# A diffusion step on one core: the broadcast of 1/rms pinned behind more products, one more gMLP group ahead, the last root on ScalarE, stores in smaller first pieces

## The chip, the cores and the metric

One core of one Trainium2 chip runs the whole program in one launch. The metric is device microseconds of that core. Of each kernel there are a few timed runs, and beside them one execution recorded by the hardware profiler, whose own time and span the tables name. The engines are called PE (TensorE), DVE (VectorE), ACT (ScalarE), POOL (GpSimd) and SP (SyncE).

## The reference, cut to what matters

128 prompt tokens and 256 latent tokens with 1024 features go through two layers. Layer 0 mixes by attention, layer 1 by a gated MLP in chunks (gMLP); after each mixer comes a gated ConvFFN. Every one of these four blocks begins with an RMS norm that is shifted and scaled by adaLN, and one RMS norm without adaLN ends the program.

```python
def rmsnorm(x, g):
    xf = x.astype(jnp.float32)
    y = xf * lax.rsqrt(jnp.mean(xf * xf, axis=-1, keepdims=True) + EPS)
    return (y * g.astype(jnp.float32)).astype(x.dtype)
...
def chunk_gmlp(h, w_in, g_v, w_s, b_s, w_out):
    ...
    z = jax.nn.gelu(h @ w_in)
    u, vv = jnp.split(z, 2, axis=-1)
    vv = layernorm(vv, g_v).reshape(B, nc, CHUNK, GMLP_GROUPS, GMLP_GROUP_DIM)
    mixed = jnp.einsum('gpq,bnqgc->bnpgc', w_s, vv) + jnp.transpose(b_s)[:, :, None]
    return (u * mixed.reshape(B, T, GMLP_WIDTH)) @ w_out
...
    for l in range(DEPTH):
        ...
        h = modulate(rmsnorm(x, norm_mix_g[l]), sm, cm)
        ...  # mix: attention in layer 0, chunk_gmlp in layer 1
        x = x + gm * mix
        h = modulate(rmsnorm(x, norm_ffn_g[l]), sf, cf)
        x = x + gf * conv_ffn(h, w_ffn_up[l], w_ffn_conv[l], b_ffn_conv[l], w_ffn_down[l])
    y_prompt = rmsnorm(x, norm_final_g)
```

## The kernel before, in words

The residual x is kept feature-major: eight tiles `x[k]` of 128 features by 384 token columns (128 prompt, 256 latent). Weights come from memory in 512 KB units (`load`, L102); ACT makes the rounded high part `hi` (L105) and DVE the rest `lo` (L106). The activations are held the same way, as `hhi` and `hlo`. One `mac` is three products on PE: high by high, low by high, high by low (L112 to L114; the text calls each a product). A block's result builds up in a PSUM bank of one of five pools; `ps_sc` has two banks, `ps_mm` three.

**A norm.** While the last residual tiles come in, ACT squares them (`square`, L289) and DVE adds the squares into `sqacc`. `norm_first` then works as follows. Four weight units are loaded; `sums` (L303) adds `sqacc` over the partitions on PE; `rsqrt` turns the sums into 1/rms `rr` (DVE L329, a power on POOL L331, one Newton step on DVE L333 to L336); `spread` (L322) copies 1/rms to all partitions with three small matmuls against `ident`; ACT copies the bank to `R` (L371). All this time PE runs 32 macs, 96 products of 386 columns, on an x that was scaled but not yet normalised (`early`), so that `late` (L385 and L386, `lt` and `lc`) can multiply their results by `R` afterwards. `modulated` then writes the normalised `hhi` and `hlo` of all eight tiles (DVE L346, ACT L348, DVE L350) for the products that follow. Norm 1 of the prediction is the one ahead of the ConvFFN of layer 0 (near 221 us), norm 2 that of the gMLP (near 497 us), norm 3 that of the ConvFFN of layer 1 (near 713 us); the norm ahead of attention is not touched.

**gMLP.** Four u groups are made from the first products, then all of v. DVE takes the layernorm statistics, `rsqrt` makes 1/std, and twelve DVE instructions normalise v (`vn`, L887). Sixteen groups follow: two banks of `ps_sc` take turns for the mixing matmuls of a group (L912, `ws` by `vn`), DVE reads the bank into `m` (L915), multiplies by the group's u (L919) and splits it. `u_part(g)` is the 24 products and the gelu (L897) of a group's u.

**The end.** After the last products x is squared once more, summed with `ones`, transposed back on PE (L958, 24 transposes into six banks), multiplied by 1/rms (ACT L967, DVE L969) and stored in six pieces of 256 KB, three issued by SP and three by ACT (L970).

Within the body a scheduler places the instructions on the engines by priorities; instructions marked `keep_in_program_order` stay where the program has them on their engine. Each engine works through its own list in order. ACT holds one table of functions at a time; a change of table is an instruction of its own in its list (ACT_TABLE_LOAD). The small vector work of the adaLN modulation (L260 on DVE) and the weight loads are spread through the program.

Of the kernel before, what the change touches and what calls it, by code (L numbers as in the profile page):

```python
# [20 lines left out]
NT = NPR + NSA
GROUPS = ((0, 0, NPR), (1, NPR, NT))
# [17 lines left out]
def backbone(ctx: ExitStack, tc: tile.TileContext, x_in, cond_in, condr_in, b_ada_in, prm_in,  # L40
             ckT_in, cv_in, wsT_in, bs_in, rpb_in, w_ada, w_ada0, w_adaT, w_qk, w_v, w_o, w_gu, w_gv,
             w_gout, w_up, w_down, y_out, skT_out, sv_out):
    nc = tc.nc
# [43 lines left out]
    make_identity(nc, ident)  # L87
    ones = cst.tile([P, P], F32, name="ones")
    nc.vector.memset(ones, 1.0)
    mhalf = cst.tile([P, 4], F32, name="mhalf")  # L90
    nc.vector.memset(mhalf, -0.5)

# [188 lines left out]
    def square(k, tag="t384", apart=True):  # L281

        sq["last"] = None
        if k == 0:
            sq["acc"] = tmp.tile([P, NT], F32, name="sqacc", tag="sqacc")
            nc.scalar.activation(sq["acc"], x[k], AF.Square)
            return
        t = tmp.tile([P, NT], F32, name="t384", tag=tag, bufs=2 if tag == "t384" else 1)
        nc.scalar.activation(t, x[k], AF.Square)  # L289
        if k < KD - 1 or not apart:  # L290
            nc.vector.tensor_tensor(sq["acc"], sq["acc"], t, ALU.add)
        else:
            sq["last"] = t
# [15 lines left out]
    def inverse(ss):  # L309

        v = tmp.tile([P, 4], F32, name="rv", tag="rv", bufs=2)
        return rsqrt(ss[:, 0:6].rearrange("p (b c) -> p b c", c=2)[:, :, 0], v[:, 0:3], 1.0 / D)

    def rms():

        return spread(inverse(sums()))

    def spread(r):

        R = bank(ps_tb)  # L320
        for b in range(3):
            mm = nc.tensor.matmul(R[:, b * P:(b + 1) * P], r[:, b:b + 1].to_broadcast([P, P]), ident,  # L322
                                  start=True, stop=True)
        return R

    def rsqrt(src, v, scale):
# [36 lines left out]
            nc.vector.scalar_tensor_tensor(hlo[:, k, a:b], x[k][:, a:b], g,  # L363
                                           hhi[:, k, a:b].bitcast(F32), ALU.mult, ALU.subtract)

    def norm_first(nxt, units):

        w = [load(u) for u in units]
        Rp = rms()
        R = tmp.tile([P, 512], F32, name="R0", tag="R0")[:, :NT]  # L370
        nc.scalar.copy(R, Rp[:, :NT])  # L371
        ps = [bank(q) for q in (ps_mm, ps_mm, ps_sc, ps_ta)[:len(w)]]
        for k in range(KD):
            for wi, p in zip(w, ps):
                mac(p[:, :NT + 2], wsel(wi, k, slice(0, P)), h(k, slice(0, NT + 2)),
                    k == 0, k == KD - 1)
        for k in range(KD):
            modulated(*nxt, k, R)
        return ps, R
# [427 lines left out]
    def ffn(l, pool, wkp, fill):  # L807
        ahi = [pool.tile([P, NT], F32R, name=f"ahi{i}") for i in range(KF)]
        alo = [pool.tile([P, NT], F32R, name=f"alo{i}") for i in range(KF)]
        allm = slice(0, P)  # L810

        def gate(i, pg, pv):
            g = conv(l, i, pg, wkp, "cg")
            v = conv(l, KF + i, pv, wkp, "cv")
            nc.scalar.activation(g, g, AF.Silu)
            nc.vector.tensor_tensor(g, g, v, ALU.mult)
            nc.scalar.copy(ahi[i], g)
            nc.vector.tensor_tensor(alo[i], g, ahi[i].bitcast(F32), ALU.subtract)

        order = [j for i in range(KF) for j in (i, KF + i)]  # L820
        ps, R = norm_first((l, SF, CF), [w_up[l, j] for j in order[:4]])

        def joined(p):
            t, c = late(p, R, wkp)
            for i, a, b in GROUPS:
                nc.scalar.activation(t[:, a:b], t[:, a:b], AF.Identity, bias=c[:, i:i + 1])
            return t

        for i in range(2):
            gate(i, joined(ps[2 * i]), joined(ps[2 * i + 1]))  # L830
        for n, j in enumerate(order[4:], 4):
            i = n // 2
            w = load(w_up[l, j], 50)
            ps.append(bank(ps_mm if i % 2 == 0 else ps_sc))
            for k in range(KD):
                mac(ps[n][:, :NT], wsel(w, k, allm), h(k), k == 0, k == KD - 1)
            if n % 2:
                gate(i, ps[n - 1], ps[n])
                if fill and 5 <= i < 21 and i % 2:
                    ada_v.run(1)  # L840
        for m in range(KD):
            ada_v.run(2 if fill else 1)
            ps = bank(ps_mm if m % 2 else ps_sc)
            for k0, kn in ((0, 8), (8, 8), (16, 6)):
                w = load(w_down[l, m, :, k0:k0 + kn, :])
                for kk in range(kn):
                    k = k0 + kk
                    mac(ps[:, :NT], wsel(w, kk, allm), (ahi[k], alo[k]), k == 0, k == KF - 1)
            residual(l, GF, m, ps, (1, SM, CM) if l == 0 else None)


    def gmlp(pool, wkp):
# [3 lines left out]
        mv = pool.tile([P, 3, 2], F32, name="mv")  # L856
        mhi = [pool.tile([P, NT], F32R, name=f"mhi{g}") for g in range(NG)]
        mlo = []
        ps, R = norm_first((1, SM, CM), [w_gu[g] for g in range(4)])
        us = []  # L860
        for g in range(4):
            t, c = late(ps[g], R, wkp)
# [28 lines left out]
        def u_part(g):  # L891
            w = load(w_gu[g])
            pu = bank(ps_mm)
            for k in range(KD):
                mac(pu[:, :NT], wsel(w, k, allm), h(k), k == 0, k == KD - 1)
            u = wkp.tile([P, NT], F32, name="u", tag="u", bufs=2)
            nc.scalar.activation(u, pu[:, :NT], AF.Gelu_apprx_tanh)  # L897
            us.append(u)

        u_part(4)
        for g in range(NG):
            if g % 2 == 0:
                ws = wkp.tile([P, 2, P], F32, name="ws", tag="ws")
# [15 lines left out]
                lo4 = pool.tile([P, 4, NT], F32R, name="mlo", tag="q", bufs=5)  # L921
            mlo.append(lo4[:, g % 4, :])
            split(mhi[g], mlo[g], m2)
            if 4 < g + 1 < NG:
                u_part(g + 1)
            if g > 3 and g % 2:
                ada_v.run(1)
        for m in range(KD):
# [22 lines left out]
    with tc.tile_pool(name="fin", bufs=1) as pool:  # L951
        turned = [[bank(q) for q in two] for two in ((ps_ta, ps_ad), (ps_sc, ps_sc), (ps_mm, ps_mm))]

        def turn(ks):
            for k in ks:
                for b in range(3):
                    o = (k % 4) * P
                    tc.keep_in_program_order(nc.tensor.transpose(  # L958
                        turned[b][k // 4][:, o:o + P], x[k][:, b * P:(b + 1) * P], ident))

        r = inverse(sums(True, lambda: turn(range(3))))
        turn(range(3, KD))
        for b in range(3):
            for half in range(2):
                y = pool.tile([P, 512], F32, name=f"y{b}{half}")
                if half:
                    nc.scalar.activation(y, turned[b][half], AF.Copy, scale=r[:, b:b + 1])  # L967
                else:
                    nc.vector.tensor_scalar(y, turned[b][half], r[:, b:b + 1], None, ALU.mult)  # L969
                (nc.sync, nc.scalar)[half].dma_start(y_out[b, :, 512 * half:512 * half + 512], y)  # L970


def _layout(inp):
# [66 lines left out]
```

## Time and profile before

| what | value |
|---|---|
| timed runs | 1000.45 us median of 3 (999.57 to 1000.53) |
| the profiled execution | 1000.85 us, of which 998.0 us is the span from first to last instruction and 2.85 us lies around it |
| PE busy | 982.9 us |
| DVE busy | 797.4 us |
| ACT busy | 476.3 us |
| POOL busy | 15.8 us |
| memory traffic | 172.94 MB, mean 173 GB/s |

The profile's page gives for each engine its busy time and share of the span, and the chain of work that ended last. Below that lie the timeline (every instruction with its start and its duration; in brackets the idle time of its engine before it and what ended it), the list of waits, and windows that sum an engine's busy time over a stretch. Rows that follow each other on an engine are drawn together as "x3" and the like. A matmul's duration of 0.34 us reaches into the next one, since matmuls are pipelined; what a product costs is the distance between two starts.

### The profile page before, as it was taken

The numbers are of one execution on the slowest core, as the hardware profiler recorded it, in microseconds if no ns is written. First come the engines' busy times: TensorE is split into PE (matmuls) and PEld (weight loads), VectorE is DVE, ScalarE is ACT, GpSimd is POOL, SyncE is SP. The second block draws the span as 40 slices with busy tenths as digits, with TensorE's granted clock in tenths as the row PEclk, the third lists the DMA queues.
The fourth block names the chain that finished last, engine by engine and source line by source line (L and its number), as shares of the span: only waits on it lengthen the run. The fifth ranks groups of instructions, "written<-read, shape, count | busy, mean of one in ns | idle before, by whom it ended". The sixth has DMA issues, their size and how long they took to land.

```text
span 998.0 us, 15825 instructions
## 1 busy us (share of the span) xinstructions
PE 982.9 (98%) x5942; PEld 934.9 (94%) x5942; DVE 797.4 (80%) x1652; ACT 476.3 (48%) x846; POOL 15.8 (2%) x31
## 2 busy tenths in 40 slices
PE   8999999999999999999999999999999999999996
PEld 5788888899999999999988899999999999999996
DVE  5668888689998889899899999687698777777552
ACT  4455656558554544333363334333485444443331
POOL 1000000000000000000000000000000000000000
PEclk9999999999999999999999999999999999999999
DMA  9886676442464445677737756465235333435521
GB/s 338 313 292 179 206 233 201 138 148 85 148 190 152 167 148 156 201 220 220 235 105 256 251 174 185 149 204 177 84 106 182 122 126 121 127 114 180 161 72 63
DMA packets 53019, 172.94 MB, mean 173 GB/s; under 512 B 6016, under 2 KB 11152, under 8 KB 52944
## 3 DMA queue, kind: packets, MB, share of 16 engines
q1 hardware_dynamic: 51840, 169.33, 53.2%
q10 hardware_dynamic: 576, 1.31, 0.3%
q0 software_dynamic: 528, 1.32, 0.3%
q8 instruction: 46, 0.75, 0.3%
q14 instruction: 29, 0.24, 0.1%
HBM read 169.31 MB, written 2.62 MB: 172 GB/s over the span
## 4 chain that ended last, share of the span: by engine, by line
PE 94%; DVE 2%; ACT 1%; issue 1%; POOL 1%; DMA 1%; POOLq 0%; SPq 0%; ACTq 0%
PE bank L113 29%; PE bank L114 29%; PE bank L112 29%; PE bank L678 1%; PE bank L629 1%; PE bank L912 1%; PE bank L661 1%; PE bank L155 1%; PE bank L199 1%; POOL ry L331 1%; DMA lo<-in_x 1%; PE bank L322 0%; DVE lo L118 0%; PE bank L303 0%; DVE bank L636 0%
## 5 line engine op out<-in xcount | busy, mean ns | idle before, releaser
L113 PE MATMUL bank<-hlo,hi 128*128 128x384 f32 (+1 forms) x976 | 330.5, 339 | 0.1
L112 PE MATMUL bank<-hhi,hi 128*128 128x384 f32 (+1 forms) x976 | 330.1, 338 | 0.0
L114 PE MATMUL bank<-hhi,lo 128*128 128x384 f32 (+1 forms) x976 | 329.9, 338 | 0.2 <-DVE lo L118 0.2
L105 ACT CAST hi<-st 128x1024 fp32r<-128x1024 f32 (+1 forms) x184 | 189.1, 1030 | 295.3 <-PE bank L113 237.9
L106 DVE TENSOR_TENSOR lo<-st,hi 128x1024 fp32r<-128x1024 f32 (+1 forms) x184 | 220.5, 1198 | 62.5 <-ACT hi L105 62.3
L114 PEld LDWEIGHTS bank<-hhi,lo 128*128 128x128 f32 x976 | 184.1, 189 | 0.7 <-DVE lo L118 0.5
L112 PEld LDWEIGHTS bank<-hhi,hi 128*128 128x128 f32 x976 | 184.0, 189 | 0.8 <-ACT hi L105 0.4
L113 PEld LDWEIGHTS bank<-hlo,hi 128*128 128x128 f32 x976 | 183.4, 188 | 0.6 <-DVE hlo L118 0.3
L114 PE MATMUL bank<-ahi,lo 128*128 128x384 f32 x352 | 118.3, 336 | 0.0
L113 PE MATMUL bank<-alo,hi 128*128 128x384 f32 x352 | 118.3, 336 | 0.0
L112 PE MATMUL bank<-ahi,hi 128*128 128x384 f32 x352 | 118.1, 336 | 0.0
L260 DVE CUSTOM_DVE_ANT_0 junk<-adb,cs 128x1024 bf16<-128x1024 f32 x72 | 87.8, 1219 | 0.5
L260 DVE CUSTOM_DVE_ANT_0 junk<-adw,cs 128x1024 bf16<-128x1024 f32 x56 | 68.3, 1220 | 0.5
L114 PEld LDWEIGHTS bank<-ahi,lo 128*128 128x128 f32 x352 | 66.2, 188 | 0.0
L113 PEld LDWEIGHTS bank<-alo,hi 128*128 128x128 f32 x352 | 66.2, 188 | 0.0
L112 PEld LDWEIGHTS bank<-ahi,hi 128*128 128x128 f32 x352 | 66.2, 188 | 0.0
L112 PE MATMUL bank<-hi,hhi 128*128 128x512 f32 x144 | 58.1, 404 | 0.4 <-ACT hhi L453 0.4
L113 PE MATMUL bank<-lo,hhi 128*128 128x512 f32 x144 | 56.9, 395 | 0.1
L114 PE MATMUL bank<-hi,hlo 128*128 128x512 f32 x144 | 56.7, 394 | 0.0
L394 DVE SCALAR_TENSOR_TENSOR x<-bank,mod,x 128x128 f32<-128x128 f32 x64 | 23.8, 413 | 33.1 <-PE bank L114 33.0
L113 PE MATMUL bank<-mlo,hi 128*128 128x384 f32 x128 | 43.6, 341 | 0.0
L112 PE MATMUL bank<-mhi,hi 128*128 128x384 f32 x128 | 43.3, 338 | 0.0
(180 smaller groups left out, 1299.8 us busy)
## 6 DMA issues: line engine op xcount, KB each, us to landing
st<-in_w_up SPq DMA_DIRECT2D x88, 512.0 KB, 3.6
adb<-in_w_adaT SPq DMA_DIRECT2D x36, 512.0 KB, 4.5
st<-in_w_down SPq DMA_DIRECT2D x32, 512.0 KB, 3.6
adw<-in_w_adaT SPq DMA_DIRECT2D x28, 512.0 KB, 3.6
adw<-in_w_ada SPq DMA_DIRECT2D x24, 512.0 KB, 5.8
st<-in_w_qk SPq DMA_DIRECT2D x16, 512.0 KB, 4.2
st<-in_w_gu SPq DMA_DIRECT2D x16, 512.0 KB, 4.4
st<-in_w_gv SPq DMA_DIRECT2D x16, 512.0 KB, 4.4
```

The source lines that it names most:

```text
L105: nc.scalar.copy(hi[:, :n], st[:, :n])
L106: nc.vector.tensor_tensor(lo[:, :n], st[:, :n], hi[:, :n].bitcast(F32), ALU.subtract)
L112: nc.tensor.matmul(out, a[0], b[0], start=start, stop=False)
L113: nc.tensor.matmul(out, a[0], b[1], start=False, stop=False)
L114: nc.tensor.matmul(out, a[1], b[0], start=False, stop=stop)
L155: nc.tensor.matmul(pa[32 * j:32 * j + 32, 0:P], cond_s[:, 4 * hf + kk, :], w[hf][:, kk, P * q:P * q + P], start=(kk == 0), stop=(kk == 3), ...
L199: nc.tensor.matmul(self.pa[32 * j:32 * j + 32, 0:256], cond_s[:, k, :], t[:, 256 * j:256 * j + 256], start=(k == 0), stop=(k == KD - 1), t ...
L260: tc.keep_in_program_order(nc.vector.tensor_tensor_reduce(self.junk, t, self.cs[c], 1.0, 0.0, ALU.mult, ALU.add, m[:, c:c + 1]))
L331: nc.gpsimd.tensor_tensor(y, v, mhalf[:, :n], ALU.pow)
L394: nc.vector.scalar_tensor_tensor(x[m][:, a:b], ps[:, a:b], mod(l, gate, m, c), x[m][:, a:b], ALU.mult, ALU.add)
L629: nc.tensor.matmul(sc[hh][:, cols], q[qp][HS[hh], qs:qs + P], k[kp][HS[hh], ks], start=i == 0, stop=i == 2)
L661: nc.tensor.transpose((ta[:, o:o + P] if g < 2 else tb[:, o - 512:o - 512 + P]), pr[:, b, g * P:g * P + P], ident)
```

## The change

Four things are changed.

1. `spread` gets a flag that marks its first matmul `keep_in_program_order`, and `norm_first` calls it in the middle of its 32 macs, behind mac number `then`: 18 in norm 1, 10 in norms 2 and 3. Before, it stood ahead of them in the program, and the scheduler placed it where it expected `rr` to be ready.
2. In the gMLP `u_part(5)` is issued ahead of the first mixing as well, every later `u_part` one group sooner, and the `u` tile has three buffers instead of two.
3. The last norm squares `x[7]` in two pieces. Its root is an ACT Sqrt (with a bias tile `eps`), with a reciprocal on DVE and the Newton step behind it, in place of the power on POOL. A Sqrt of one column after the last gate of the second ConvFFN brings the table in ahead of time.
4. The first 128 tokens are written out as two pieces of 256 columns for each half. There are eight stores, seven of them on SP and the last one on ACT.

The diff, without lines that only move names:

```diff
-        nc.scalar.activation(t, x[k], AF.Square)
+        for _, a, b in GROUPS if k == KD - 1 and apart else ((0, 0, NT),):
+            nc.scalar.activation(t[:, a:b], x[k][:, a:b], AF.Square)
...
-    def rms():
-
-        return spread(inverse(sums()))
-
-    def spread(r):
+    def spread(r, pin=False):
...
+            if pin and not b:
+                tc.keep_in_program_order(mm)
...
-    def norm_first(nxt, units):
+    def norm_first(nxt, units, then):
...
-        Rp = rms()
+        r = inverse(sums())
         R = tmp.tile([P, 512], F32, name="R0", tag="R0")[:, :NT]
-        nc.scalar.copy(R, Rp[:, :NT])
...
+                then -= 1
+                if then == 0:
+                    Rp = spread(r, True)
+                    nc.scalar.copy(R, Rp[:, :NT])
...
-        ps, R = norm_first((l, SF, CF), [w_up[l, j] for j in order[:4]])
+        ps, R = norm_first((l, SF, CF), [w_up[l, j] for j in order[:4]], 10 if l else 18)
...
+        if l:
+
+            nc.scalar.activation(root[:, 3:4], ahi[KF - 1].bitcast(F32)[:, 0:1], AF.Sqrt, scale=0.0)
...
-        ps, R = norm_first((1, SM, CM), [w_gu[g] for g in range(4)])
+        ps, R = norm_first((1, SM, CM), [w_gu[g] for g in range(4)], 10)
...
-            u = wkp.tile([P, NT], F32, name="u", tag="u", bufs=2)
+            u = wkp.tile([P, NT], F32, name="u", tag="u", bufs=3)
...
         u_part(4)
+        u_part(5)
...
-            if 4 < g + 1 < NG:
-                u_part(g + 1)
+            if 5 < g + 2 < NG:
+                u_part(g + 2)
...
-        r = inverse(sums(True, lambda: turn(range(3))))
+        ss = sums(True, lambda: turn(range(3)))[:, 0:6].rearrange("p (b c) -> p b c", c=2)[:, :, 0]
         turn(range(3, KD))
...
+        nc.scalar.activation(root[:, 0:3], ss, AF.Sqrt, bias=eps, scale=1.0 / D)
+        nc.vector.tensor_scalar(v, ss, 1.0 / D, EPS, ALU.mult, ALU.add)
+        nc.vector.reciprocal(y0, root[:, 0:3])
+        nc.vector.tensor_tensor(t, y0, y0, ALU.mult)
+        nc.vector.scalar_tensor_tensor(t, t, -0.5, v, ALU.mult, ALU.mult)
+        nc.vector.scalar_tensor_tensor(r, t, 1.5, y0, ALU.add, ALU.mult)
+        pieces = [(0, 0, 256), (0, 256, 512), (1, 0, 512), (2, 0, 512)]
+        for i, (b, c0, c1) in enumerate(pieces):
             for half in range(2):
...
+                q = nc.scalar if half and i == 3 else nc.sync
+                q.dma_start(y_out[b, :, 512 * half + c0:512 * half + c1], y)
```

Line numbers shift a little with the edit: the products are L113 to L115 afterwards, the split of the weights L106 and L107, `spread` L320, `late` L389 and L390, `vn` L894, the mixing L920 and `m` L923.

The order of the instructions moves further than the diff says, since the scheduler places the rest around the pinned ones. Three places follow. In the rows the numbers behind the names are those of buffers: they tell tiles of one name apart.

PE in norm 1, before: the products of the unnormalised x (banks 2662 to 2665 take turns), with the spread of `rr` between two products of one mac.

```order
L114 MATMUL bank_2664<-hhi_131,lo_2634 128x386
L112 MATMUL bank_2665<-hhi_131,hi_2638 128x386
L322 MATMUL bank_2656<-ident_120,rr_2654 128x128 x3
L113 MATMUL bank_2665<-hlo_132,hi_2638 128x386
L114 MATMUL bank_2665<-hhi_131,lo_2640 128x386
```

The same place now (banks 2658 to 2661).

```order
L115 MATMUL bank_2658<-hhi_132,lo_2623 128x386
L113 MATMUL bank_2659<-hhi_132,hi_2627 128x386
L114 MATMUL bank_2659<-hlo_133,hi_2627 128x386
L115 MATMUL bank_2659<-hhi_132,lo_2629 128x386
L320 MATMUL bank_2716<-ident_120,rr_2655 128x128 x3
L113 MATMUL bank_2660<-hhi_132,hi_2633 128x386
```

The spread is row 1179 of PE's list before and row 1187 now, eight products later; between the sums and the spread stood 12 products, and now 20. In norms 2 and 3 there were 8, and now 14.

DVE at the end of norm 1's modulation, before: `lt` and `lc` free the banks of the first products, `hlo` of tile 7 (from `t384_2811`) is written in two pieces, and `lo_2908` and `lo_2955` are low parts of weight units.

```order
L385 TENSOR_TENSOR lt_2824<-bank_2663,R0_2660 128x384
L386 COPY lc_2825<-bank_2663 128x2
L350 SCALAR_TENSOR_TENSOR hlo_132<-t384_2811,mod0_129,hhi_131 128x128
L106 TENSOR_TENSOR lo_2908<-st_2905,hi_2906 128x1024
L350 SCALAR_TENSOR_TENSOR hlo_132<-t384_2811,mod0_129,hhi_131 128x256
L106 TENSOR_TENSOR lo_2955<-st_2952,hi_2953 128x1024
L801 SCALAR_TENSOR_TENSOR cg_2830<-lt_2818,prm_111,cg_2830 128x127
```

The same place now (tile 7 is `t384_2812`, the first of the two weight parts `lo_2909`).

```order
L350 SCALAR_TENSOR_TENSOR hlo_133<-t384_2805,mod0_130,hhi_132 128x256
L350 SCALAR_TENSOR_TENSOR hlo_133<-t384_2812,mod0_130,hhi_132 128x128
L350 SCALAR_TENSOR_TENSOR hlo_133<-t384_2812,mod0_130,hhi_132 128x256
L390 COPY lc_2826<-bank_2659 128x2
L107 TENSOR_TENSOR lo_2909<-st_2906,hi_2907 128x1024
L805 SCALAR_TENSOR_TENSOR cg_2831<-lt_2819,prm_111,cg_2831 128x127
```

The first weight part now stands behind both pieces of `hlo`, and the second behind the `cg` work. On PE the first product that reads `lo_2908` was row 1256, 77 rows behind the spread; the first that reads `lo_2909` is row 1258, 71 rows behind it. A little later on ACT, the cast of the high part `hi_3032` (before, `hi_3031`) stood directly behind the first gate's Silu and now stands behind two more activations that read `lt_2847` and `lc_2848`; its first product on PE was row 1326 and is now row 1282.

PE at the first mixing of the gMLP, now (`bank_6132` collects u 5, `bank_6224` u 6; the mixing of a group is one row of three matmuls).

```order
L115 MATMUL bank_6132<-hhi_132,lo_6129 128x384
L920 MATMUL bank_6163<-ws_6159,vn_5338 128x128 x3
L920 MATMUL bank_6173<-ws_6159,vn_5338 128x128 x3
L113 MATMUL bank_6224<-hhi_132,hi_6219 128x384
L114 MATMUL bank_6224<-hlo_133,hi_6219 128x384
L115 MATMUL bank_6224<-hhi_132,lo_6221 128x384
L113 MATMUL bank_6224<-hhi_132,hi_6219 128x384
L114 MATMUL bank_6224<-hlo_133,hi_6219 128x384
L920 MATMUL bank_6186<-ws_6182,vn_5338 128x128 x3
L920 MATMUL bank_6195<-ws_6182,vn_5338 128x128 x3
```

Before, 41 products stood between the start of the u groups and the first pair of mixings, and 24 between the first and the second pair; now it is 48 and 5. On DVE, two adaLN reductions (L260) and one weight part (L106) stood between 1/std's first Newton step and the twelve `vn`; now none of these do, and one such reduction stands ahead of the statistics' end instead.

More of the change, by code (lines that the diff above doesn't have):

```diff
@@ L89, in backbone @@
     nc.vector.memset(ones, 1.0)
+    root = cst.tile([P, 4], F32, name="root")
     mhalf = cst.tile([P, 4], F32, name="mhalf")
@@ L959, in turn @@
                         turned[b][k // 4][:, o:o + P], x[k][:, b * P:(b + 1) * P], ident))
-        r = inverse(sums(True, lambda: turn(range(3))))
+        ss = sums(True, lambda: turn(range(3)))[:, 0:6].rearrange("p (b c) -> p b c", c=2)[:, :, 0]
         turn(range(3, KD))
-        for b in range(3):
+        eps = tmp.tile([P, 1], F32, name="eps", tag="eps")
+        nc.vector.memset(eps, EPS)
+        v, y0, t, r = (pool.tile([P, 3], F32, name=n) for n in ("v", "y0", "t", "r"))
+        nc.scalar.activation(root[:, 0:3], ss, AF.Sqrt, bias=eps, scale=1.0 / D)
[6 more added lines that the diff above has]
+        for i, (b, c0, c1) in enumerate(pieces):
             for half in range(2):
-                y = pool.tile([P, 512], F32, name=f"y{b}{half}")
+                y = pool.tile([P, c1 - c0], F32, name=f"y{i}{half}")
+                src = turned[b][half][:, c0:c1]
                 if half:
-                    nc.scalar.activation(y, turned[b][half], AF.Copy, scale=r[:, b:b + 1])
+                    nc.scalar.activation(y, src, AF.Copy, scale=r[:, b:b + 1])
                 else:
-                    nc.vector.tensor_scalar(y, turned[b][half], r[:, b:b + 1], None, ALU.mult)
-                (nc.sync, nc.scalar)[half].dma_start(y_out[b, :, 512 * half:512 * half + 512], y)
+                    nc.vector.tensor_scalar(y, src, r[:, b:b + 1], None, ALU.mult)
+                q = nc.scalar if half and i == 3 else nc.sync
+                q.dma_start(y_out[b, :, 512 * half + c0:512 * half + c1], y)
 def _layout(inp):
```

## The prediction

> **What bounds the kernel now.** I read the page first, then the list of waits, the timeline around each place that the diff touches, and a window behind norm 1.
>
> ```profile
> span 998.0 us, 15825 instructions
> ...
> PE 982.9 (98%) x5942; PEld 934.9 (94%) x5942; DVE 797.4 (80%) x1652; ACT 476.3 (48%) x846; POOL 15.8 (2%) x31
> ...
> PE 94%; DVE 2%; ACT 1%; issue 1%; POOL 1%; DMA 1%; POOLq 0%; SPq 0%; ACTq 0%
> ```
>
> PE is busy for 98% of the span and carries 94% of the chain that ends last. No product is removed, so the change can win only where PE stands still, and behind the last product. Where it stands still, the waits of PE name two lines of this change:
>
> ```profile
> PE bank L322 <- DVE rr L336: 1.4, 3, 0.6
> ...
> PE bank L912 <- DVE vn L887: 0.9, 1, 0.9
> ```
>
> In each of three norms the spread (L322) comes up before `rr` is there, 1.4 us together; the first mixing of the gMLP waits 0.9 us for `vn`. That is nearly all there is to win in the body.
>
> **Part 1, norm 1.** The waits in their places:
>
> ```profile
> 221.09 0.33 PE L112 MATMUL bank<-hhi,hi 128*128 128x386 f32 x1
> ...
> 222.03 0.91 PE L322 MATMUL bank<-ident,rr 128*128 128x128 f32 x6 [0.61 <-DVE rr L336]
> ...
> 497.16 0.91 PE L322 MATMUL bank<-ident,rr 128*128 128x128 f32 x6 [0.34 <-DVE rr L336]
> ...
> 713.13 0.91 PE L322 MATMUL bank<-ident,rr 128*128 128x128 f32 x6 [0.42 <-DVE rr L336]
> ```
>
> The cost of a product comes from the window behind norm 1, quoted below: 13.00 us for 75 starts, 0.173 us each; with 386 columns it is nearer 0.175. From 221.09 to 222.03 are 0.94 us where a product takes 0.175, so 0.77 us are lost; the wait in brackets is 0.16 less because it counts from the modelled end. By the same 0.16, norms 2 and 3 lose 0.50 and 0.58. With eight (six) more products ahead, 1.40 (1.05) us of work, the spread no longer waits: all three losses go, 1.85 us.
>
> But the spread was also the start of another chain: R, `modulated`, `late`. It now starts 1.40 us later against PE's products: in norm 1 at 221.09 + 0.175 + 1.40 = 222.67 instead of 222.03, that is 0.64 later by the clock, while PE is 0.77 ahead. Whether this comes back depends on how far ahead of PE the chain runs afterwards.
>
> ```profile
> 232.00:245.00 13.00, 13.00 (x75) 12.73 (x74) 12.91 (x31) 11.53 (x22) 0.00 (x0) 1.00 0.28 93
> ...
> 234.89 1.22 DVE L106 TENSOR_TENSOR lo<-st,hi 128x1024 fp32r<-128x1024 f32 x1
> 236.03 0.48 DVE L350 SCALAR_TENSOR_TENSOR hlo<-t,mod,hhi 128x256 fp32r<-128x256 f32 x1
> 236.16 0.44 PE L114 MATMUL bank<-hhi,lo 128*128 128x384 f32 x1
> ...
> 236.62 0.39 PE L113 MATMUL bank<-hlo,hi 128*128 128x384 f32 x1
> ```
>
> In the window DVE (third figure) works 12.91 of 13 us: it has no idle time in which to catch up. The weight part `lo` ends at 236.11 and its first product starts at 236.16; `hlo` of the last tile ends at 236.51 and its product starts at 236.62. The slack is 0.05 and 0.11 us. A chain that comes 1.40 us later against PE must stop PE here.
>
> How long, from the new order. `lo_2909` stands behind both pieces of `hlo`, so it is later by the second piece's step (236.42 - 236.03 = 0.39) and by the chain's 0.64: 236.11 + 0.39 + 0.64 = 237.14, and its product, row 1258, can start at 237.19. Before, row 1258 started at 236.62 (the L113 row above). PE is thus 0.57 us behind the kernel before instead of 0.77 ahead: of the 0.77, 1.34 has come back.
>
> The next thing late is a cast on ACT.
>
> ```profile
> 236.42 1.22 DVE L106 TENSOR_TENSOR lo<-st,hi 128x1024 fp32r<-128x1024 f32 x1
> ...
> 240.33 0.53 ACT L815 ACTIVATE cg<-cg 128x384 f32<-128x384 f32 x1
> ...
> 240.65 0.15 DVE L386 COPY lc<-bank 128x2 f32<-128x2 f32 x1
> ```
>
> The groups of the stretch from 234 to 245 us give the two `lt` activations (busy us, mean ns):
>
> ```profile
> L826 ACT ACTIVATE lt<-lt,lc 128x256 f32<-128x256 f32 x4 | 2.0, 499 | 0.0
> ...
> L826 ACT ACTIVATE lt<-lt,lc 128x128 f32<-128x128 f32 x4 | 1.6, 390 | 0.0
> ```
>
> DVE's gate work follows 237.14 now and 237.64 before (the second `lo`, 236.42 + 1.22, has left this place), so Silu comes 0.50 earlier, 239.83 to 240.36; the two `lt` activations take about 0.39 + 0.50 less 0.1 of overlap, to 241.15, and the cast of 1.04 follows to about 242.1. Its first product, row 1282, is 24 products behind row 1258: 237.19 + 24 x 0.175 = 241.39. That is a stop of about 0.7 us. Before, that product was row 1326, 44 products (7.7 us) later. PE is then 0.57 + 0.7 = 1.3 us behind. For stops behind that I know only bounds, nothing and the 0.6 by which the chain was late at 237; I take the middle, 0.3. Norm 1: 1.6 us slower, between 0.6 (only the first stop) and 1.9.
>
> **Norms 2 and 3.** The nearest step behind norm 2 is the copy that frees a bank for the v products:
>
> ```profile
> 510.24 0.15 DVE L386 COPY lc<-bank 128x2 f32<-128x2 f32 x1
> ...
> 511.27 0.40 PE L112 MATMUL bank<-hi,hhi 128*128 128x512 f32 x1
> ```
>
> It ends 0.88 us ahead of its product; the chain shifts by 1.05, so 0.2 comes back and 0.3 of 0.50 is won. Behind norm 3 I found no step with less than 1.05 in hand, so 0.6 is won there. Ends for both together: -1.1 and, if all comes back, 0.
>
> **Part 2, gMLP.**
>
> ```profile
> 577.28 0.34 PE L112 MATMUL bank<-hhi,hi 128*128 128x384 f32 x1
> ...
> 579.15 0.17 DVE L329 TENSOR_SCALAR rv<-mv 128x3 f32<-128x3 f32 x1
> ...
> 581.23 0.16 DVE L333 TENSOR_TENSOR rt<-ry 128x3 f32<-128x3 f32 x1 [0.74 <-POOL ry L331]
> ...
> 584.32 0.33 PE L113 MATMUL bank<-hlo,hi 128*128 128x384 f32 x1
> 584.93 5.57 DVE L887 TENSOR_SCALAR vn<-vn,mv,rr 128x512 f32<-128x512 f32 x12
> 585.52 1.62 PE L912 MATMUL bank<-ws,vn 128*128 128x128 f32 x12 [0.88 <-DVE vn L887]
> 586.91 0.42 PE L114 MATMUL bank<-hhi,lo 128*128 128x384 f32 x1
> ...
> 590.40 1.14 DVE L915 SCALAR_TENSOR_TENSOR m<-bank,prm,bs 128x384 f32<-128x384 f32 x2
> ```
>
> From 584.32 to 585.52 are 1.20 us for one product: 1.03 lost. Seven more products ahead (48 against 41) are 1.2 us, and `vn` starts earlier, so this loss goes. What is late next: the second pair of mixings needs a bank of `ps_sc` that `m` of the first pair (L915) must empty, and on DVE `m` stands behind all twelve `vn`. Before, 24 products (4.2 us) lay between the pairs; now five. Counted from the first u product: PE reaches the second pair after 48 x 0.175 = 8.4, the first pair's 586.91 - 585.52 = 1.39 and 5 x 0.175, at 10.7. On DVE `rv` came at 579.15 - 577.28 = 1.87, now about 1.3 later for the reduction ahead of it (the two that have left took 584.93 - 581.23 = 3.70 with one `lo` of 1.14 among them, so 1.28 each); `rt` 2.08 later as before, two small steps 0.4, then 5.57 of `vn` and 0.57 of one `m`: 11.8. PE stops for about 1.1 us. Gain 1.03, loss 1.1: 0.1 slower, between -1.03 (no stop) and +0.5.
>
> **Parts 3 and 4, the end.**
>
> ```profile
> 988.75 0.16 DVE L329 TENSOR_SCALAR rv<-bank 128x3 f32<-128x3 f32 x1 [1.48 <-PE bank L303]
> ...
> 990.33 0.16 DVE L336 SCALAR_TENSOR_TENSOR rr<-rt,ry 128x3 f32<-128x3 f32 x1
> 990.59 1.26 ACT L967 ACTIVATE y<-bank,rr 128x512 f32<-128x512 f32 x2 [2.11 <-DVE rr L336]
> 990.60 2.07 DVE L969 TENSOR_SCALAR y<-bank,rr 128x512 f32<-128x512 f32 x3
> 991.31 0.92 ACTq L970 DMA_DIRECT2D out_y<-y  x2
> ```
>
> Of the stores, the view of the tile `y` gives SP's issues (shortest, median, longest ns); of a table load, the groups give its time; and the timeline gives ACT's first work after the last gate, with its idle time before:
>
> ```profile
> L970 SPq DMA_DIRECT2D out_y<-y x3: 343/347/428, 991.4 to 992.7; - x3
> ...
> L865 ACT ACT_TABLE_LOAD x1 | 1.3, 1283 | 0.0
> ...
> 903.15 1.05 ACT L105 CAST hi<-st 128x1024 fp32r<-128x1024 f32 x1 [2.91 <-PE bank L113]
> ```
>
> The sums are ready at 988.75. The Sqrt takes about 0.3 (an estimate: the 128-column row of L826, 390 ns, less 125 columns at the 0.85 ns that its two rows differ by), to 989.06; five DVE steps at about 0.2 (three columns take 0.16, and the next waits for the result) end at 990.03, and y starts at about 990.14 instead of 990.60. A first piece of 256 columns is done 0.2 sooner besides, so the first store leaves 0.66 before 991.31. Squaring in two pieces brings nothing, as PE's transposes fill that time. The table load (1.28) falls where ACT idles 2.91 us and costs nothing. But seven stores now leave one after the other on SP at 0.35 to 0.43 each, the first four with half the bytes, so part of the lead is lost: the end moves by -0.66 at best and -0.2 at worst; I take -0.45.
>
> The Trainium skill speaks on both points: "ScalarE: Activation LUTs", What ACT_TABLE_LOAD costs, counts 2.66 us for each switch of set with its drain, where the row shows 1.28 for the load; by either it hides or nearly hides in that idle time. "DMA: Bandwidth & Descriptors", Issuing engines are not separate DMA queues, says that several issuers save only the issuing time, since all share 16 DMA engines; by it the whole 0.66 would be kept and the sum below would be 0.2 less. No run here shows the new order of stores yet.
>
> **Sum.** Norm 1 +1.6, norms 2 and 3 -0.3 and -0.6, gMLP +0.1, end -0.45: +0.35 us on the profiled run's 1000.85, so 1001.2. The median of the runs shown is 1000.45, 0.40 below that run: 1000.8.
>
> **The rivals.** A measurement of this kernel can tell about 0.2% (2.0 us) from no change.
>
> *Nothing comes back (faster).* The scheduler's other moves refill the slack at 236 us and DVE empties the gMLP's banks in time. Then -1.85 - 1.03 - 0.66 = -3.5: 997.0. For it: in the window behind norm 1 PE is busy for 13.00 of 13.00 us before, beside the same DVE. Against it: the 0.05 and 0.11 us at 236 us. Chance 0.20.
>
> *Half comes back.* Only the first stop of norm 1 (+0.6), no stop at the bank (-1.03), the rest as forecast: 0.6 - 0.9 - 1.03 - 0.45 = -1.8: 998.7. Chance 0.22.
>
> *The bank wait dominates (slower).* If PE reaches the first pair just as the first `vn` is done, the second pair waits for eleven more `vn` and an `m`: 5.57 x 11/12 + 0.57 - 1.39 - 0.88 = 3.4, a net of +2.4 instead of +0.1: 1003.1. It decides from a wait of about 2.8 us on. For it: the order of DVE's list. Against it: the 8.4 us of products that now stand ahead. Chance 0.08.
>
> *The root does not do what it says.* If a second table load (1.28) fell between the sums and the Sqrt, the end would be 0.8 slower instead of 0.45 faster: 1002.1. For it: two functions with tables of their own in one program. Against it: ACT's new list holds one more ACT_TABLE_LOAD, at the Sqrt after the last gate, and none behind it. By the Trainium skill's 2.66 it would be 1003.5. Chance 0.05.
>
> **How the numbers follow.** The forecast has 0.45, mostly between 999.8 and 1001.9. Faster than 998.45: the first rival and a quarter of the second, 0.26; slower than 1002.45: the third and a little of the fourth, 0.09; the rest, 0.65, is no change. The range runs from 996.8, just below the first rival, to 1002.3, which leaves out the third.
>
> **What would show it.** Right: no L320 wait of more than 0.1 in three norms; a PE wait of 0.7 to 1.8 us on DVE `lo` L107 within 16 us of norm 1's spread and one on ACT `hi` L106 some 5 us on; a wait of about 1.1 of the second L920 pair on DVE `m` L923; y near 0.46 sooner after the sums. Wrong: no such PE waits at 232 to 256 us (then the first rival), or a PE wait above 2.8 in the gMLP.

## The result and the profile after

| | before | after |
|---|---|---|
| median, us (6 runs each) | 1000.42 (999.57 to 1001.89) | 1004.07 (1003.83 to 1004.30) |
| ratio | | 1.0037 (95% interval 1.0026 to 1.0047) |
| span of the profiled execution, us | 998.0 | 1001.8 |

The change costs 3.65 us, where 0.35 was forecast. The page of the changed kernel and its list of PE waits, to set beside those of before:

```profile
span 1001.8 us, 15829 instructions
...
PE 987.2 (99%) x5941; PEld 938.9 (94%) x5942; DVE 798.3 (80%) x1655; ACT 480.4 (48%) x851; POOL 15.0 (1%) x30
...
PE 92%; DVE 4%; ACT 1%; DMA 1%; issue 0%; POOL 0%; SPq 0%; POOLq 0%; ACTq 0%
```

```profile
PE bank L115 <- DVE lo L107: 1.5, 2, 0.9
...
PE bank L920 <- DVE m L923: 0.9, 1, 0.9
...
PE bank L113 <- ACT hi L106: 0.5, 1, 0.5
```

The waits moved as forecast: L320 waits for `rr` no longer, and the mixing no longer for `vn`. In their place stand the three that the prediction named: a low part on DVE, a cast on ACT, and the bank that `m` has to empty. But PE's waits on these lines add up to 2.9 us now and 2.3 before (1.4 + 0.9), and PE's busy time rose by 4.3 us (987.2 against 982.9) with the same products. The waits can't account for 3.65 us. To see what does, I set the starts of the nth matmul of both traces beside each other and took the time between two of them:

| matmuls | what lies there | before, us | after, us | difference |
|---|---|---|---|---|
| start to 1500 | attention | 203.45 | 203.80 | +0.35 |
| 1500 to 1800 | norm 1 and the 35 us behind it | 53.20 | 55.32 | +2.12 |
| 1800 to 2600 | first half of ConvFFN 0 | 140.25 | 140.23 | -0.02 |
| 2600 to 3100 | `w_down` of ConvFFN 0 | 86.69 | 88.31 | +1.62 |
| 3100 to 3500 | norm 2, u and v of the gMLP | 83.96 | 83.59 | -0.37 |
| 3500 to 4300 | mixing, output of the gMLP | 138.15 | 137.93 | -0.22 |
| 4300 to 4600 | norm 3 | 52.72 | 52.10 | -0.62 |
| 4600 to 5400 | first half of ConvFFN 1 | 140.20 | 140.26 | +0.06 |
| 5400 to 5900 | `w_down` of ConvFFN 1 | 86.67 | 88.34 | +1.67 |
| 5900 to the end | | 12.7 | 11.9 | -0.8 |

The trace of the changed kernel lacks one matmul record ahead of number 1500, so that its nth matmul from there on is one further along: 0.17 us of the first row's difference, and of the last row's, is that and no work. Two rows were in no step of the prediction: the `w_down` products of both ConvFFNs, 3.3 us together, spread evenly and with no wait among them. Windows inside these stretches show it as fewer starts (the count behind PE's busy time) in the same time at the same granted clock (third figure from the right). Before:

```profile
410.00:480.00 70.00, 70.00 (x406) 70.00 (x405) 64.11 (x120) 25.14 (x41) 0.00 (x0) 1.00 0.72 226
920.00:970.00 50.00, 50.00 (x290) 50.00 (x289) 32.07 (x52) 16.79 (x21) 0.00 (x0) 1.00 0.43 127
```

After:

```profile
410.00:480.00 70.00, 70.00 (x398) 70.00 (x397) 63.72 (x118) 24.79 (x39) 0.00 (x0) 1.00 0.69 216
920.00:970.00 50.00, 50.00 (x285) 50.00 (x284) 30.42 (x48) 18.08 (x23) 0.00 (x0) 1.00 0.45 137
```

PE is busy all the time in both, and a product takes 70 / 406 = 0.172 us before and 70 / 398 = 0.176 after. The mean step in the traces is 173.3 and 176.7 ns; 1056 products read `ahi` or `alo`, which makes 3.5 us. Products on `hhi` and `hlo` kept their step (175.3 and 175.4 ns).

The change does nothing there. What it does is bring two new tiles, `root` (16 bytes of each partition) and `eps` (4 bytes). The allocator gives each 32 bytes, and everything allocated behind them moves. From the compiled programs, the places of the tiles in bytes (modulo 64 is what a division by 64 leaves over):

| kernel | `hi`, `lo` (first) | modulo 64 | `ahi0` | modulo 64 | distance of `ahi0` from `hi`, modulo 64 |
|---|---|---|---|---|---|
| before | 47072, 67552 | 32 | 147328 | 0 | 32 |
| after | 47104, 67584 | 0 | 147392 | 0 | 0 |

**Theory A:** where the operands lie to each other sets the step of a product. **Theory B:** the place of the weights does. **Theory C:** the new order of the instructions does, and places don't matter.

### The profile page after: what moved, and what is told of

Same layout as the page of the kernel before. It is cut to its first block, busy times and chain, and to the rows that moved or that the text cites. A ratio compares the mean times of both kernels' runs of the same rounds, so it can differ in the third digit from the quotient of the medians.

```text
span 1001.8 us, 15829 instructions
## 1 busy us (share of the span) xinstructions
PE 987.2 (99%) x5941; PEld 938.9 (94%) x5942; DVE 798.3 (80%) x1655; ACT 480.4 (48%) x851; POOL 15.0 (1%) x30
## 4 chain that ended last, share of the span: by engine, by line
PE 92%; DVE 4%; ACT 1%; DMA 1%; issue 0%; POOL 0%; SPq 0%; POOLq 0%; ACTq 0%
PE bank L115 28%; PE bank L113 28%; PE bank L114 28%; PE bank L682 1%; PE bank L633 1%; PE bank L665 1%; PE bank L920 1%; PE bank L156 1%; PE bank L200 1%; DMA lo<-in_x 1%; DVE vn L894 1%; DMA st<-in_w_up 0%; DVE lo L119 0%; DVE lo L107 0%; DVE junk L261 0%
## 5 line engine op out<-in xcount | busy, mean ns | idle before, releaser
L115 PE MATMUL bank<-hhi,lo 128*128 128x384 f32 (+1 forms) x976 | 329.9, 339 | 1.7 <-DVE lo L107 1.5
L106 ACT CAST hi<-st 128x1024 fp32r<-128x1024 f32 (+1 forms) x184 | 189.2, 1031 | 295.8 <-PE bank L114 239.9
L113 PE MATMUL bank<-hhi,hi 128*128 128x384 f32 (+1 forms) x976 | 330.6, 339 | 0.5 <-ACT hi L106 0.5
L107 DVE TENSOR_TENSOR lo<-st,hi 128x1024 fp32r<-128x1024 f32 (+1 forms) x184 | 220.4, 1198 | 68.9 <-ACT hi L106 68.3
L115 PEld LDWEIGHTS bank<-hhi,lo 128*128 128x128 f32 x976 | 184.1, 189 | 2.7 <-DVE lo L107 2.2
L113 PEld LDWEIGHTS bank<-hhi,hi 128*128 128x128 f32 x976 | 184.0, 189 | 1.5 <-ACT hi L106 0.8
L115 PE MATMUL bank<-ahi,lo 128*128 128x384 f32 x352 | 119.0, 338 | 0.0
L113 PE MATMUL bank<-ahi,hi 128*128 128x384 f32 x352 | 118.8, 338 | 0.0
L115 PEld LDWEIGHTS bank<-ahi,lo 128*128 128x128 f32 x352 | 66.0, 187 | 0.0
L113 PEld LDWEIGHTS bank<-ahi,hi 128*128 128x128 f32 x352 | 65.9, 187 | 0.0
L113 PE MATMUL bank<-hi,hhi 128*128 128x512 f32 x144 | 58.1, 404 | 0.4 <-ACT hhi L457 0.4
L115 PE MATMUL bank<-hi,hlo 128*128 128x512 f32 x144 | 56.7, 394 | 0.0
L113 PE MATMUL bank<-mhi,hi 128*128 128x384 f32 x128 | 43.9, 344 | 0.0
L115 PE MATMUL bank<-mhi,lo 128*128 128x384 f32 x128 | 43.3, 338 | 0.0
```

The lines of the kernel that those rows point to most:

```text
L106: nc.scalar.copy(hi[:, :n], st[:, :n])
L107: nc.vector.tensor_tensor(lo[:, :n], st[:, :n], hi[:, :n].bitcast(F32), ALU.subtract)
L113: nc.tensor.matmul(out, a[0], b[0], start=start, stop=False)
L115: nc.tensor.matmul(out, a[1], b[0], start=False, stop=stop)
```

## The experiments

Times are medians against the kernel before on the same chip, ratios with 95% intervals.

**Root alone.** Before, with one line more:

```diff
+    root = cst.tile([P, 4], F32, name="root")
+    nc.gpsimd.memset(root, 0.0)
     mhalf = cst.tile([P, 4], F32, name="mhalf")
```

> The kernel before with one more 16-byte tile, root, set once by POOL and read by nothing. The tile moves the weights' tiles hi and lo by 32 bytes in each partition, and the ConvFFN's activations ahi and alo by 32 bytes as well, so that the distance between the two, taken modulo 64 bytes, stays 32 as in the kernel before (in the changed kernel it is 0). Theory A (PE's distance between two products depends on how the two operands lie to each other modulo 64 bytes): the products on ahi and alo stay at 0.173 us, the time stays within 0.5 us of the kernel before. Theory B (it depends on where the weights lie): 0.177 us as in the changed kernel, 1056 products x 0.0034 = 3.5 us slower. Theory C (the changed order of instructions slows the products, places do not matter): no change.

Measured: 1000.76 against 1000.28, ratio 1.0005 (0.9996 to 1.0014), no change. The windows in both `w_down` stretches:

```profile
410.00:480.00 70.00, 70.00 (x406) 70.00 (x405) 64.63 (x119) 25.94 (x41) 0.00 (x0) 1.00 0.70 229
920.00:970.00 50.00, 50.00 (x291) 50.00 (x290) 32.40 (x51) 17.42 (x23) 0.00 (x0) 1.00 0.43 132
```

406 and 291 starts, as before. The weights lie where they lie in the changed kernel, so theory B falls.

**Eps alone.**

```diff
+        eps = tmp.tile([P, 1], F32, name="eps", tag="eps")
+        nc.gpsimd.memset(eps, EPS)
         r = inverse(sums(True, lambda: turn(range(3))))
```

> The kernel before with one more 4-byte tile, eps, where the changed kernel has it, set once by POOL and read by nothing. It moves ahi and alo by 32 bytes and leaves hi and lo where they were: the distance modulo 64 becomes 0 as in the changed kernel, with the order of the products unchanged. Theory A (relative place): the products on ahi and alo go from 0.173 to 0.177 us, 1056 x 0.0034 = 3.5 us slower, near 1003.9 us, less up to 0.6 us that the gMLP's output products may win. Theory B (place of the weights): no change. Theory C (order of instructions): no change.

Measured: 1003.45 against 1000.28, ratio 1.0031 (1.0019 to 1.0042): 3.2 us for a tile of four bytes that nobody reads.

```profile
410.00:480.00 70.00, 70.00 (x399) 70.00 (x398) 63.67 (x119) 25.46 (x41) 0.00 (x0) 1.00 0.69 224
920.00:970.00 50.00, 50.00 (x285) 50.00 (x284) 31.39 (x49) 17.93 (x23) 0.00 (x0) 1.00 0.45 137
```

399 and 285 starts, the slow step in both. The order of the products is the old one, so theory C falls too. Root alone and eps alone both give POOL one instruction more, and only one of the two is slow, so that instruction is not the cause.

**The changed kernel, tiles in their old places.**

```diff
-    root = cst.tile([P, 4], F32, name="root")
-    mhalf = cst.tile([P, 4], F32, name="mhalf")
+    both = cst.tile([P, 8], F32, name="both")
+    mhalf, eps, root = both[:, 0:3], both[:, 3:4], both[:, 4:8]
...
-        eps = tmp.tile([P, 1], F32, name="eps", tag="eps")
```

> The changed kernel, with root and eps put into the 32 bytes that the tile mhalf already takes, so that every other tile lies where it lay in the kernel before. Theory A and B (places): the products on ahi and alo are back at 0.173 us, the time falls by 3 to 3.5 us from 1004.1 to about 1000.6 to 1001.0, that is no change against the kernel before. Theory C (order of instructions): 1004.1 as the changed kernel.

Measured: 1000.95 against 1000.28, ratio 1.0006 (0.9997 to 1.0015); 406 starts in the first window. All four parts of the change together, without the move, cost 0.7 us and can't be told from no change.

**Both tiles, old order; and a third place.** Root and eps as above in the kernel before; and the changed kernel with `eps` as `[P, 16]`, 64 bytes.

> The kernel before with both tiles, root and eps, set once by POOL and read by nothing: all tiles lie where they lie in the changed kernel up to the last norm, and the order of the products is that of the kernel before. If the places alone make the difference: 0.177 us for the products on ahi and alo in both ConvFFNs, near 1003.4 to 1003.9 as with eps alone. If eps alone was slow for another reason: 1000.4.

> The changed kernel with eps as a tile of 64 bytes instead of 4: ahi, alo and the gMLP's tiles move by 32 bytes more, so that ahi and alo lie 32 modulo 64 from the weights again, at places that no other run has. If that distance decides here: 0.173 us and about 1000.9. If the kernel before's own places are needed: 1003.5 to 1004.1.

Measured: 1003.63 against 1000.16, ratio 1.0033 (1.0021 to 1.0046), for the first; 1000.54, ratio 1.0003 (0.9994 to 1.0012), for the second. Their rows, the first kernel's two and the second's two:

```profile
410.00:480.00 70.00, 70.00 (x398) 70.00 (x398) 63.65 (x119) 25.36 (x41) 0.00 (x0) 1.00 0.70 225
920.00:970.00 50.00, 50.00 (x285) 50.00 (x284) 31.41 (x49) 17.71 (x23) 0.00 (x0) 1.00 0.44 136
...
410.00:480.00 70.00, 70.00 (x406) 70.00 (x405) 64.63 (x120) 24.89 (x40) 0.00 (x0) 1.00 0.70 220
920.00:970.00 50.00, 50.00 (x290) 50.00 (x289) 32.39 (x51) 17.80 (x23) 0.00 (x0) 1.00 0.43 134
```

32 bytes more of nothing make the changed kernel 3.5 us faster. Both came as theory A says. The first also explains the gMLP row of the table above: with the old order and the new places, matmuls 3500 to 4300 take 137.76 us against 138.15, so the 0.22 us that the changed kernel gains there come from the places and not from part 2.

**Can the place be made better?** `hhi` has a row of 1544 bytes, so its eight parts lie at eight distances modulo 64. Two kernels give them one:

```diff
-    hhi = hp.tile([P, KD, NT + 2], F32R, name="hhi")
-    hlo = hp.tile([P, KD, NT + 2], F32R, name="hlo")
+    hhi = hp.tile([P, KD, 400], F32R, name="hhi")[:, :, 8:8 + NT + 2]
+    hlo = hp.tile([P, KD, 400], F32R, name="hlo")[:, :, 8:8 + NT + 2]
```

The other begins at 4 instead of 8, and has `ahi` and `alo` 1600 bytes apart, begun 48 bytes in.

> The kernel before with the eight parts of hhi and hlo 1600 bytes apart instead of 1544, and begun 32 bytes in, so that every part lies 32 modulo 64 from the weights, as ahi and alo do in the kernel before; now each part lies 8 further than the last, and the products go through all eight distances. Theory A (the distance modulo 64 sets the product's time): the products on hhi and hlo of 384 columns fall from 0.175 on average to 0.1733, 2928 of them x 0.0017 = 5 us faster, near 995.3. Theory A2 (it is the change of distance from one product to the next, or the tile, and not the distance): no change or slower.

> As the run with parts 1600 bytes apart, but with hhi, hlo, ahi and alo all 16 modulo 64 from the weights (ahi and alo 1600 bytes apart as well). In the trace of the kernel before the part of hhi at this distance has the shortest products (169, 175 and 172 ns for the three of a mac, mean 172.0). Theory A: hhi and hlo 2928 x 0.003 = 8.8 us, ahi and alo 1056 x 0.0013 = 1.4 us: about 10 us faster, near 990. Theory A2: no gain, or a loss as with the changed kernel's distance of 0.

Measured: 1003.81, ratio 1.0032 (1.0020 to 1.0043), and 1003.95, ratio 1.0032 (1.0019 to 1.0044), against 1000.48. Both are slower, where theory A expected 5 and 10 us faster; so theory A in its simple form fails: a distance alone does not give the time. A2 had no gain or a loss, but the two runs don't show that its reason is the right one. In the first, the two `w_down` stretches differ, with the same tiles, places and order of products:

```profile
410.00:480.00 70.00, 70.00 (x406) 70.00 (x405) 64.63 (x120) 25.78 (x41) 0.00 (x0) 1.00 0.73 229
920.00:970.00 50.00, 50.00 (x284) 50.00 (x284) 30.86 (x49) 18.04 (x23) 0.00 (x0) 1.00 0.46 137
```

406 starts are the fast step and 284 the slow one. By the starts of the nth matmul this kernel loses 1.5 us from norm 3 through the first half of ConvFFN 1 (matmuls 4300 to 5400) and 1.7 in its `w_down`, and nothing in ConvFFN 0. In the trace the fast train goes 173, 173, 174 ns over and over, the slow one here 178, 175, 180, 174, 177, 175. A train of equal products keeps one rhythm for 80 us and more; which of them it falls into depends on the places, but not on them alone. The second kernel has a step between the two:

```profile
410.00:480.00 70.00, 70.00 (x404) 70.00 (x403) 64.33 (x121) 25.78 (x40) 0.00 (x0) 1.00 0.73 225
920.00:970.00 50.00, 50.00 (x289) 50.00 (x288) 30.95 (x50) 18.02 (x23) 0.00 (x0) 1.00 0.45 137
```

Its mean step on `ahi` and `alo` is 174.4 ns, and the one on `hhi` and `hlo` 176.3 against 175.3.

**The parts by themselves**, with all tiles in their old places: part 1 (the spread), parts 3 and 4 (the end), part 2 (the gMLP); each is the kernel before with that part of the diff.

> The kernel before with the first part of the change alone (the spread of 1/rms pinned behind 18, 10 and 10 macs), places as before. From the trace of the changed kernel: norm 1 costs about 2.1 us net (three PE waits on DVE lo, ACT hi and DVE lo of 0.75, 0.63 and 1.10 us take the place of one of 0.77), norms 2 and 3 win 0.4 and 0.6: 1.1 us slower, near 1001.5. If the waits behind norm 1 come from the other parts of the change and not from the pinned spread: 1.9 us faster, near 998.5.

> The kernel before with parts 3 and 4 alone (root on ScalarE, eight stores), root and eps in the 32 bytes of mhalf so that no other tile moves. From the trace of the changed kernel the end behind the last product is 0.8 us shorter: near 999.6. The prediction's own term was 0.45 (0.2 to 0.66). If the shorter end in the changed kernel came from its body: no change.

> The kernel before with part 2 alone (the gMLP's u one group further ahead), places as before. If a bank wait of about 0.9 to 1.1 us takes the place of the wait of 0.9 for vn, as in the changed kernel: no change, 1000.3. If that bank wait belongs to the order that parts 1 and 2 make together: up to 1.0 us faster, near 999.3, and no PE wait of the mixing on DVE m.

| run | us | before | ratio |
|---|---|---|---|
| part 1 | 1001.76 | 1000.28 | 1.0013 (1.0004 to 1.0022) |
| parts 3 and 4 | 999.64 | 1000.48 | 0.9991 (0.9983 to 1.0000) |
| part 2 | 1000.17 | 1000.48 | 0.9996 (0.9987 to 1.0005) |

Part 1 loses 1.5 us. Its list of PE waits has the stops behind norm 1 without any other part of the change:

```profile
PE bank L114 <- DVE lo L106: 2.4, 2, 1.8
...
PE bank L914 <- DVE vn L889: 0.9, 1, 0.9
PE bank L112 <- ACT hi L105: 0.5, 1, 0.5
```

By the starts of the nth matmul, norms 2 and 3 win 0.58 and 0.64 in this run. Part 2 alone trades its wait for one of the same length, on `m`:

```profile
PE bank L913 <- DVE m L916: 0.9, 1, 0.9
```

**What won, put together**: the spread pinned in norms 2 and 3 only, the new end, no move (norm 1 is called with 0, which leaves its spread unpinned and ahead of the macs); and the same with 16 for norm 1.

```diff
+        if not then:
+            Rp = spread(r)
+            nc.scalar.copy(R, Rp[:, :NT])
...
+        ps, R = norm_first((l, SF, CF), [w_up[l, j] for j in order[:4]], 10 if l else 0)
```

> The kernel before with what won in the runs so far: the spread pinned in norms 2 and 3 alone (in norm 1 it stays where the scheduler had it), the new end, no move of any tile. The steps measured add up to -0.6 (norm 2), -0.6 (norm 3) and -0.8 (end): 2.0 us faster, near 998.4. If the parts don't add up, or the scheduler moves norm 1 all the same: 999 to 1001.

> The kernel before with the spread pinned behind 16 macs in norm 1 instead of 18, 10 in norms 2 and 3, the new end, no move of any tile. Two products more than before stand ahead of norm 1's spread, not eight, and the order on DVE and ACT behind it stays that of the kernel before (the first low part ahead of the second piece of hlo; the cast ahead of lt). Theory D (a later spread comes back one for one behind norm 1, since DVE is full there): norm 1 neither wins nor loses, PE waits 0.4 for rr and about 0.3 more near 236 us: within 0.3 us of the run with norm 1 unpinned. Theory E (what costs in norm 1 is the new order on DVE, ACT and PE, not the lateness): 0.3 us faster than that run, no wait near 236.

Measured: 998.30, ratio 0.9980 (0.9971 to 0.9989), and 998.01, ratio 0.9979 (0.9971 to 0.9988), against 1000.16. Both beat both kernels, by 1.9 and 2.2 us over the kernel before. They differ by less than the runs can tell, so theories D and E are not decided by the time. With 16, the list of waits has 0.3 for `rr` in norm 1 and nothing near 236 us, as theory E has it. But the list leaves out what the starts show: PE comes out of this spread 0.35 us further ahead of the kernel before than it went in, and has lost 0.31 of it again by 238 us, where its products start right behind DVE's low part, as they did before:

```profile
236.07 1.22 DVE L108 TENSOR_TENSOR lo<-st,hi 128x1024 fp32r<-128x1024 f32 x1
...
237.35 0.45 PE L116 MATMUL bank<-hhi,lo 128*128 128x384 f32 x1
```

The low part ends at 237.29, 0.06 us ahead of the start. What the spread gave comes back nearly one for one with the order on DVE unchanged, which is theory D for the first stop.

## Why the prediction was wrong

The forecast was no change, 1000.8 us; the same change without the move of the tiles measures 1000.95, and the changed kernel 1004.07. **The step that failed** is a term that the sum does not have. The prediction opens with "No product is removed, so the change can win only where PE stands still, and behind the last product", and its sum goes through norms, gMLP and end; the cost of a product, 0.173 to 0.175 us, is taken as the same before and after. The two new tiles were so put at nothing, without a reason. They move `ahi` and `alo` against the weights, and 1056 products take 3.3 ns longer each: 3.2 us with `eps` alone, 3.5 with both. The range ended at 1002.3, because no case in it touched PE's step.

That 1000.95 without the move lies so near to 1000.8 is in part luck. In the trace of that run norm 1 costs 1.1 us more than forecast, and norm 2 and the end give 0.6 us more than forecast.

The other steps, against the runs:

| step | forecast, us | measured, us | from |
|---|---|---|---|
| norm 1 | +1.6 | +2.4 to +3.3 | matmuls 1590 to 1800, four traces |
| norm 2 | -0.3 | -0.58 | part 1 alone |
| norm 3 | -0.6 | -0.64 | part 1 alone |
| gMLP | +0.1 | +0.1 | part 2 alone, matmuls 3500 to 4300 |
| the end | -0.45 | -0.75 and -0.84 | parts 3 and 4 alone, trace and time (the interval of the time reaches 0) |
| places of the tiles | not seen | +3.2 to +3.5 | eps alone, both tiles |

**Norm 1: the first two stops right, the third too small.** The stops of the changed kernel:

```profile
222.60 0.83 PE L320 MATMUL bank<-ident,rr 128*128 128x128 f32 x6
...
236.92 0.44 PE L115 MATMUL bank<-hhi,lo 128*128 128x384 f32 x1 [0.59 <-DVE lo L107]
...
241.85 0.45 PE L113 MATMUL bank<-hhi,hi 128*128 128x384 f32 x1 [0.46 <-ACT hi L106]
...
251.48 0.44 PE L115 MATMUL bank<-hhi,lo 128*128 128x384 f32 x1 [0.94 <-DVE lo L107]
```

The spread was forecast for 222.67, the product behind the low part for 237.19, the one behind the cast for about 242.1; they came at 222.60, 236.92 and 241.85. Four traces have this order: after, tiles in their old places, part 1 alone, `eps` with 64 bytes. Counted from matmul 1590, just ahead of the spread, PE is 0.42 us behind the kernel before after the first stop and 1.15 to 1.16 after the second in all four, where 0.57 and 1.3 were forecast. (The row of the first table has +2.12 instead of +2.4 because the trace of after wins 0.25 ahead of the spread.) The third stop, for which the prediction took the middle of 0 and 0.6, waits 0.94 here and costs 1.2, 1.5, 2.1 and 1.6 us in the four. DVE and ACT show why:

```profile
249.08 0.56 DVE L822 TENSOR_TENSOR alo<-cg,ahi 128x384 fp32r<-128x384 f32 x1 [0.66 <-ACT ahi L821]
249.55 0.34 DVE L807 SCALAR_TENSOR_TENSOR cv<-bank,prm,cv 128x127 f32<-128x127 f32 x1
249.81 0.47 DVE L805 SCALAR_TENSOR_TENSOR cv<-bank,prm,cv 128x255 f32<-128x255 f32 x1
250.21 1.22 DVE L107 TENSOR_TENSOR lo<-st,hi 128x1024 fp32r<-128x1024 f32 x1
```

```profile
247.59 1.05 ACT L106 CAST hi<-st 128x1024 fp32r<-128x1024 f32 x1 [0.88 <-DMA st<-in_w_up]
248.54 0.51 ACT L821 CAST ahi<-cg 128x384 fp32r<-128x384 f32 x1
```

The low part stands behind gate work on DVE; that waited 0.66 for a cast on ACT, and that cast stands behind another one, which had waited 0.88 for the transfer of its weight unit. The transfer was late by the new order. A unit arrives in one of three `st` buffers, and SP issues the next transfer when DVE's low part has read a buffer. The issues, before and after:

```profile
237.70 0.33 SPq L102 DMA_DIRECT2D st<-in_w_up  x1
...
242.22 0.33 SPq L103 DMA_DIRECT2D st<-in_w_up  x1
243.36 0.33 SPq L103 DMA_DIRECT2D st<-in_w_up  x1
```

Before, the second low part ended at 237.64 and the transfer left at 237.70. Now this low part stands behind the `cg` work and more, and the transfer leaves at 242.22, the one behind it at 243.36. The last lands 4.2 us later, just ahead of the cast at 247.59. With the tiles in their old places it took 4.5 us and the cast waited 1.05, and in part 1 alone 5.1 and 1.50; the third stop grew with it. So 0.6, the lateness of the chain, was no upper bound: the prediction followed the low parts to their products, but not to the buffers that they free. With 16 macs the low part kept its place, the transfer left at 238.88 and no cast waited. What eight products' delay would do in the old order was not tried.

**Norm 2** was forecast to give 0.2 back at the `lc` copy; nothing came back.

**gMLP: right.** The wait for the bank was forecast at 1.1 and is 0.91; in part 2 alone the nth matmul starts 0.12 later behind the mixing than ahead of it.

```profile
586.34 5.56 DVE L894 TENSOR_SCALAR vn<-vn,mv,rr 128x512 f32<-128x512 f32 x12
589.19 1.50 PE L920 MATMUL bank<-ws,vn 128*128 128x128 f32 x12
591.82 1.13 DVE L923 SCALAR_TENSOR_TENSOR m<-bank,prm,bs 128x384 f32<-128x384 f32 x2
592.48 1.60 PE L920 MATMUL bank<-ws,vn 128*128 128x128 f32 x12 [0.91 <-DVE m L923]
```

The first pair no longer waits, and the second waits for the first `m`, which follows twelve `vn`.

**The end: somewhat better than forecast.**

```profile
990.58 0.34 PE L115 MATMUL bank<-ahi,lo 128*128 128x384 f32 x1
...
993.12 0.26 ACT L975 ACTIVATE root<-bank,eps 128x3 f32<-128x3 f32 x1 [0.32 <-PE bank L305]
...
994.36 2.19 DVE L989 TENSOR_SCALAR y<-bank,r 128x256 f32<-128x256 f32 x4
...
994.87 3.59 SPq L991 DMA_DIRECT2D out_y<-y  x7
...
L991 SPq DMA_DIRECT2D out_y<-y x7: 348/423/711, 994.9 to 997.7; - x7
```

From Sqrt to y are 1.24 us, where from `rv` to y there were 1.85 (988.75 to 990.60). The seven issues of SP take 3.59 us from the first to the end of the last, and 0.35 to 0.71 each, the median 0.42, where 0.35 to 0.43 was forecast. The last leaves 7.2 us behind the last product, and before the last store left 6.8 behind it; yet the trace ends 11.2 us behind that product and before 11.8 (998.0 less 986.15). The stores now land 2.0 us after their issue, where it was 3.4 (medians). In the trace of parts 3 and 4 alone it ends at 11.1. The table load hid as forecast:

```profile
902.48 0.51 ACT L821 CAST ahi<-cg 128x384 fp32r<-128x384 f32 x1
903.01 1.28 ACT L847 ACT_TABLE_LOAD   x1
904.30 0.20 ACT L847 ACTIVATE root<-ahi 128x1 f32<-128x1 f32 x1
905.98 1.05 ACT L106 CAST hi<-st 128x1024 fp32r<-128x1024 f32 x1 [1.47 <-PE bank L114]
```

ACT still idles 1.47 us behind it. The 2.66 us that the Trainium skill gives for a switch with its drain ("ScalarE: Activation LUTs", What ACT_TABLE_LOAD costs) are not seen here: from the end of the cast to the start of the Sqrt, 902.99 to 904.30, are 1.3 us.

**The rivals.** "Half comes back" and "Nothing comes back" had norm 1 too cheap: its stops came. "The bank wait dominates" came near the time, 1003.1, by a cause that did not occur.

## What to carry to other kernels

When a change adds or resizes a tile, count the tiles that move as part of the change: set the places of the operands of the busiest engine side by side in both compiled programs, and if a kernel whose waits went as planned is still slower, count the starts of its main instruction in equal windows. Try the change with the new tile folded into an old one before judging its other parts. A step that feeds a full engine can't be put off for nothing: what the wait gave returns behind it. And a step that is moved back on such an engine has to be followed to the buffer that it frees, and to the transfer that waits for the buffer.

## What the hardware showed that was not expected

The step of equal products of 128 by 384 has several steady values, on average 173.3 and 176.7 ns in most runs and 174.4 in one, at a granted clock of 1.00, with PE and its weight loads busy throughout. In every kernel that left the rows of `hhi` at 1544 bytes, the step on `ahi` and `alo` was the short one where their distance to the weights is 32 modulo 64 (nine kernels), and the long one where it is 0 (the changed kernel, eps alone, both tiles). The tiles allocated behind `eps` move together with `ahi` and `alo`; that it is the distance of a product's own two operands that counts, and not that of some other pair, is likely but not shown. And the second window of the first kernel with 1600-byte rows has a distance of 32 and the long step. What else picks the rhythm stays open. With the natural 1544-byte rows of `hhi` single steps run from 169 to 185 ns, with a mean of 175.
